# Seven plain pairs ahead of the block products, and modulation work spread anew, in a two-layer HGRN2 and gated-MLP backbone

## The chip, the cores and the metric

The kernel runs on one core of one Trainium2 chip. The metric is the device time of one execution in microseconds. TensorE (PE) multiplies matrices into eight PSUM banks, VectorE (DVE) and ScalarE (ACT) work elementwise, GpSimd (POOL) does a few small steps, and SyncE (SP) issues every DMA from one queue, in order. Each engine takes its instructions in the order in which they were laid down when the kernel was built; a semaphore makes an instruction wait for another engine or a DMA, and what stands behind it on its engine waits too.

## The reference, cut to what matters

Two layers work on 512 latent tokens of width 1024 and, in the first layer, on 256 context tokens as well. Each layer is a SwiGLU feed-forward, a token mixer (a bidirectional gated recurrence in the first, a chunked spatial MLP in the second), and another feed-forward. Every one of these has a modulated input and a modulated residual:

```
m = silu(cond) @ w_mod + b_mod                  # nine rows of 1024 for each layer and condition
h = x * (1 + m[3k+1]) + m[3k]                   # input of sub-layer k
g, u = split(h @ w_in);  y = (silu(g) * u) @ w_out
x = layer_norm(alpha * x + m[3k+2] * 0.5 * y)   # no 0.5 for the mixer
```

The context has a condition of its own (c_ctx), so a row of m that both streams use is computed for both conditions, "x" and "c". The feed-forward has 2816 hidden features, 22 blocks of 128. All products are in fp32, each made of three matmuls of rounded parts: high by high, high by low, low by high (L152, L153, L154).

## The kernel before

**Operands.** A weight tile is loaded to `raw` (3 buffers, 512 KB each) and split by ScalarE (L139, high part) and VectorE (L140, low part) into `w` (6 buffers). Token operands are split in the same way; `xa` holds the high and low part of all 768 tokens in one tile.

**Start.** Each of the eight 128-row slices k of the tokens needs two modulation dots (L171, one VectorE instruction of 1024 columns that multiplies a weight tile with the condition row and sums). As the slices come in, the three first feed-forward pairs (f = 0, 1, 2; a pair is the gate block and the up block of 128 hidden features) are summed in six PSUM banks (`products`, L1168). Behind them come the context's condition row, its tokens (1 MB) and its 16 dots, which use the same weight tiles (L1225 to L1231). Then the first three pairs are evacuated (`evac`, L1036: ScalarE silu, VectorE product to `h`, store to `hd` in DRAM), three more "plain" pairs are computed on the 512 latent tokens, and `context_operand` (L1234) scales and splits the context's tokens.

**Block products.** The other 16 pairs go over all 768 tokens in a form with seven instead of eight products (`by_sums`, L1053; `seven`, L669): gate and up, halves of the features and halves of the tokens are added and subtracted beforehand, the sums of the tokens are f4 to f7 (`sum_steps`, L1007), and every product is four slices of three matmuls with 384 columns. For the six plain pairs the 256 context tokens follow at the end.

**Output product.** `BothOut` (L1073) multiplies the stored pairs with the second weight. For each half of the 1024 output columns it goes over 11 units; a unit is one weight tile and two stored pairs (`hl`, 384 KB each), 36 matmuls of 512 columns. The tokens x come in at its start (six tiles, L1113). At the end it normalises, builds the operand of the recurrence, starts its values (psv) and stores x (L341, L342).

**Modulation.** The other rows of m are made on the side. `mod_task` (L173 on) is a generator: each step loads one 512 KB tile into `mraw` (2 buffers) and takes one dot for each condition; after eight steps it adds the bias, and a gate row (rows 2, 5, 8) is also transposed by TensorE (L187, pg) and stored. `mod_step(n)` adds n to a credit and runs as many steps as it holds; `made(key)` runs what is missing at once. Before, the queue holds rows (layer, row) (0, 2), (0, 4), (0, 3) for both conditions and (0, 5), (0, 7), (0, 6), (0, 8), (1, 2) for x: 64 steps. A block pair and a context pair give one step each, a unit of the output product two (its last units of either half give none), and L1280 makes the rest.

**Second layer's modulation.** The second feed-forward's output product makes rows (1, 1) and (1, 0) at one step a unit; the third's makes (1, 4), (1, 3), (1, 5) at 1.5.

**Pools.** SBUF is a stack of pools; a tile may take the place of an earlier pool's tile and then waits for that tile's last reader. `first` (the start's tiles) is closed before `hp` (silu, h) is opened in its place. In the second feed-forward `sp2` (rawu, e, sc of the block form) lies where `blocks` was, the tiles of token blocks from which f4 to f7 are summed.

The order on each engine comes from a scheduler when the kernel is built, by the program's order and its own estimate of times.

Of the kernel before, what the change touches and what calls it, by code (L numbers as in the profile page):

```python
# [11 lines left out]
F32 = mybir.dt.float32  # L12
# [30 lines left out]
NPLAIN = 6  # L43
# [31 lines left out]
def backbone_kernel(  # L75
# [905 lines left out]

    def new_xa():

        xa = xap.tile([P, 2, KD, TA], F32R, tag="xa", name="xa")
        return xa, xa[:, :, :, :T], xa[:, :, :, T:]
# [12 lines left out]
    class FeedBoth(Forms, FeedIn):  # L998
# [37 lines left out]
        def evac(self, hp, f, psg, psu, c0, c1):  # L1036
            c = slice(c0, c1)
            s = hp.tile([P, TA], F32, tag="silu", name="silu", bufs=1)
            nc.scalar.activation(s[:, c], psg[:, : c1 - c0], AF.Silu)
            h = hp.tile([P, TA], F32, tag="h", name="h", bufs=3)  # L1040
            nc.vector.tensor_tensor(h[:, c], psu[:, : c1 - c0], s[:, c], ALU.mult)
            nc.sync.dma_start(hd[f][:, c], h[:, c])
# [10 lines left out]
        def by_sums(self, hp, sp, f, early=None):  # L1053
            sc = sp.tile([P, 4, TS], F32, tag="sc", name="sc", bufs=1)
            s = hp.tile([P, TA], F32, tag="silu", name="silu", bufs=1)
            h = hp.tile([P, TA], F32, tag="h", name="h", bufs=3)
            pa, pe, pc, pb = self.seven(
                self.xa, sp, self.src(2 * f), self.src(2 * f + 1), [sc[:, i, :] for i in range(4)], early
            )
            if pb is not None:  # L1060
                nc.vector.tensor_tensor(s[:, TS:], sc[:, 3, :], pb, ALU.subtract)
            nc.vector.tensor_tensor(s[:, :TS], pa, sc[:, 0, :], ALU.add)
            nc.scalar.activation(s[:, :TS], s[:, :TS], AF.Silu)
            nc.vector.tensor_tensor(h[:, TS:], sc[:, 3, :], sc[:, 1, :], ALU.subtract)
            nc.vector.tensor_tensor(h[:, :TS], pe, sc[:, 2, :], ALU.add)
            if pb is not None:
                nc.scalar.activation(s[:, TS:], s[:, TS:], AF.Silu)
            else:
                nc.scalar.activation(s[:, TS:], pc, AF.Silu, scale=-1.0)
            nc.vector.tensor_tensor(h, h, s, ALU.mult)  # L1070
            nc.sync.dma_start(hd[f], h)
# [82 lines left out]
    with ExitStack() as e_sc:  # L1154
# [3 lines left out]
        f0.blk = early.enter_context(swap("blk")).tile([P, KD, TA], F32, name="blk")  # L1158
        with sbuf(name="first", bufs=1) as fp:
# [4 lines left out]
            xf = fp.tile([P, T], F32, name="xf")  # L1164
# [33 lines left out]
            for k in range(KD):  # L1198
# [20 lines left out]
                if k == 0:  # L1219
                    for _ in first:  # L1220
                        pass
                elif k < 4:
                    f0.load((2, 2, 1)[k - 1])
            products(KD - 1, staged)
            srow["c"] = silu_row(fp, "c")  # L1225
            nc.sync.dma_start(f0.blk[:, :, T:], ctxT.rearrange("k p t -> p k t"))
            for k in [*range(KD // 2, KD), *range(KD // 2)]:
                for ch in (1, 0):
                    mod_dot(fp, acc_c[:, k, ch : ch + 1], row(k, ch), srow["c"])
            ccols = const.tile([P, KD, 2], F32, name="ccols")  # L1230
# [3 lines left out]
        def context_operand():  # L1234
            for k in range(KD):
                ct = f0.blk[:, k, T:]
                nc.vector.tensor_scalar(ct, ct, ccols[:, k, 1:2], ccols[:, k, 0:1], ALU.mult, ALU.add)
                if k % 2:
                    ks = slice(k - 1, k + 1)
                    split(xmc[:, 0, ks, :], xmc[:, 1, ks, :], f0.blk[:, ks, T:])  # L1240
                    yield

        with sbuf(name="hp", bufs=1) as hp, sbuf(name="ru", bufs=1) as ru, sbuf(name="f47", bufs=1) as f47:
            for f in range(3):
                f0.evac(hp, f, f0.pss[2 * f], f0.pss[2 * f + 1], 0, T)
            ctx_steps = context_operand()
            for f in range(3, NPLAIN):
                f0.plain(hp, f, xm, 0, T)
                if f > 3:
                    for _ in range(2):  # L1250
                        next(ctx_steps, None)
            for _ in ctx_steps:
                pass
# [8 lines left out]
            for f in range(NPLAIN, NF):  # L1262
                f0.by_sums(hp, sp, f, steps if f == NPLAIN else None)
                if f == NPLAIN:
# [5 lines left out]
                    for l, ch in ((0, 5), (0, 7), (0, 6), (0, 8), (1, 2)):  # L1270
                        queue_mod(modq, srow, l, ch, ["x"])
                mod_step(1)
            for f in range(NPLAIN):
                f0.plain(hp, f, xmc, T, TA)
                mod_step(1)
        with bpools() as bp, sbuf(name="hl", bufs=1) as hl:
# [3 lines left out]
            for l, ch in ((0, 5), (0, 7), (0, 6), (0, 8), (1, 2)):  # L1280
                made((l, ch, "x"))


    with sbuf(name="hgo", bufs=1) as hgo, ExitStack() as late:
# [302 lines left out]
        with bpools() as bp:  # L1587
            xm = new_xm(xmp, "xm", T)
            n = KD * T
            flat = xap.tile([P, 2 * KD * TA], F32, tag="xa", name="blocks")[:, 2 * KD * TA - n :]  # L1590
# [7 lines left out]
    with sbuf(name="sp2", bufs=1) as sp, bpools() as bp, sbuf(name="hp2", bufs=1) as hp:  # L1598
# [11 lines left out]
        scraps(sp, 1, (1, 0))  # L1610
        op.run(bp, None, 1)
# [235 lines left out]
```

## Time and profile before

| What | Value |
|---|---|
| Time before, median of 3 runs (lowest to highest) | 2454.4 us (2454.2 to 2454.79) |
| The profiled execution's own time | 2452.35 us |
| Its span, first to last instruction | 2450.2 us |
| Granted TensorE clock, mean of the span | 0.993 |
| Share of the span busy: PE, DVE, ACT | 97%, 81%, 48% |
| Mean DMA rate over the span | 145 GB/s |

The page and the views group instructions by line, engine and tile names, "out<-in". In the list of waits a row has the waiting engine and tile, what released it, and the sum, the count and the longest of the waits. A timeline row has the start from the span's beginning, the duration, the engine, the line, the instruction and its tiles, and in brackets the idle time before it and its releaser. A row of windows has the stretch, its length, the busy time of PE, weight load, DVE, ACT and POOL (with counts), the granted clock, the busy share of the DMA engines and GB/s. Matmuls overlap, so the pace is read from start to start, not from a duration. Waits of engines other than TensorE cost nothing while TensorE is fed.

### The profile page before, as it was taken

Reading aid. Unit: us, or ns where it says so; the run is one execution under the profiler, and the core shown is the slowest. Engines: PE = TensorE matmul, PEld = TensorE weight load, DVE = VectorE, ACT = ScalarE, POOL = GpSimd, SP = SyncE. Lnnn points to the kernel's source line nnn. Section 1 sums busy time; section 2 is a strip of 40 time slices with the busy share of each in tenths; the row PEclk is TensorE's granted clock in tenths of the full one; section 3 lists DMA queues with packets and bytes.
Section 4 is the critical chain, followed back from the end, with each engine's and each line's share of the span. In section 5 each row is a group of like instructions: output and inputs, shape, how many; then the busy total and the mean of one; then the engine's idle time right before and its main releaser. Section 6 shows DMA issues by size and latency. Waiting matters only on the chain.

```text
span 2450.2 us, 37518 instructions
## 1 busy us (share of the span) xinstructions
PE 2383.5 (97%) x14787; PEld 2188.1 (89%) x14787; DVE 1985.2 (81%) x3173; ACT 1180.3 (48%) x1835; POOL 37.5 (2%) x57
## 2 busy tenths in 40 slices
PE   7899999996999999999999999999999999999998
PEld 5799998885889888899988999988999988999987
DVE  7987886866488886888796988898889877988785
ACT  4444442333354452555643655534566634555641
POOL 0000000000000000000000000000000000000000
PEclk9999999998999999999999999999999999999999
DMA  8444378953211113433474333474322365333452
GB/s 308 153 144 143 129 249 312 311 208 123 84 52 61 61 52 103 151 121 104 139 236 147 113 107 104 150 258 141 129 85 89 127 214 174 131 118 104 139 163 77
DMA packets 107889, 356.27 MB, mean 145 GB/s; under 512 B 12424, under 2 KB 14528, under 8 KB 107712
## 3 DMA queue, kind: packets, MB, share of 16 engines
q1 hardware_dynamic: 107712, 353.88, 42.8%
q8 instruction: 115, 1.88, 0.3%
q14 instruction: 62, 0.51, 0.1%
HBM read 332.57 MB, written 21.26 MB: 144 GB/s over the span
## 4 chain that ended last, share of the span: by engine, by line
PE 54%; DVE 3%; DMA 1%; ACT 0%; issue 0%; POOL 0%; SPq 0%; DVEq 0%; POOLq 0%
PE y L154 6%; PE y L153 6%; PE y L152 6%; PE psc L152 5%; PE psc L154 5%; PE psc L153 5%; PE pse L154 3%; PE pse L152 3%; PE pse L153 3%; PE psa L154 1%; PE psa L153 1%; PE psa L152 1%; PE pscs L1710 1%; PE pvc L154 1%; PE pvc L152 1%; PE pvc L153 1%
## 5 line engine op out<-in xcount | busy, mean ns | idle before, releaser
L139 ACT ACTIVATE w<-raw 128x1024 fp32r<-128x1024 f32 (+3 forms) x393 | 371.7, 949 | 359.3 <-DMA raw<-in_ffn_w_out 102.8
L140 DVE TENSOR_TENSOR w<-raw,w 128x1024 fp32r<-128x1024 f32 (+3 forms) x393 | 425.9, 1088 | 138.5 <-ACT w L139 137.7
L152 PE MATMUL y<-w,hs 128*128 128x512 f32 x984 | 383.4, 390 | 1.1 <-ACT hs L139 1.1
L154 PE MATMUL y<-w,hs 128*128 128x512 f32 x984 | 382.5, 389 | 1.6 <-DVE hs L140 1.6
L153 PE MATMUL y<-w,hs 128*128 128x512 f32 x984 | 382.7, 389 | 0.7 <-DVE w L140 0.7
L154 PEld LDWEIGHTS y<-w,hs 128*128 128x128 f32 x984 | 184.7, 188 | 40.8 <-DVE hs L140 2.0
L152 PEld LDWEIGHTS y<-w,hs 128*128 128x128 f32 x984 | 184.7, 188 | 39.5 <-ACT hs L139 1.5
L153 PEld LDWEIGHTS y<-w,hs 128*128 128x128 f32 x984 | 184.7, 188 | 39.0 <-DVE w L140 1.1
L152 PE MATMUL pse<-f,w 128*128 128x256 f32 (+1 forms) x688 | 202.0, 294 | 5.6 <-ACT sc L732 3.3
L152 PE MATMUL psc<-f,w 128*128 128x256 f32 (+1 forms) x688 | 201.8, 293 | 1.7 <-ACT sc L732 1.7
L154 PE MATMUL pse<-f,w 128*128 128x256 f32 (+1 forms) x688 | 202.3, 294 | 0.2 <-DVE w L140 0.2
L153 PE MATMUL pse<-f,w 128*128 128x256 f32 (+1 forms) x688 | 201.6, 293 | 0.0
L153 PE MATMUL psc<-f,w 128*128 128x256 f32 (+1 forms) x688 | 201.3, 293 | 0.0
L154 PE MATMUL psc<-f,w 128*128 128x256 f32 (+1 forms) x688 | 201.2, 292 | 0.0
L732 ACT ACTIVATE sc<-psc 128x256 f32<-128x256 f32 (+1 forms) x238 | 96.3, 404 | 150.8 <-PE psc L154 137.0
L152 PE MATMUL psc<-xm,w 128*128 128x256 f32 x548 | 156.1, 285 | 0.0
L154 PE MATMUL psc<-xm,w 128*128 128x256 f32 x548 | 155.1, 283 | 0.0
L153 PE MATMUL psc<-xm,w 128*128 128x256 f32 x548 | 155.0, 283 | 0.0
L140 DVE TENSOR_TENSOR w<-rawu,w 128x1024 fp32r<-128x1024 f32 x86 | 105.2, 1223 | 54.2 <-ACT w L139 53.6
L152 PEld LDWEIGHTS pse<-f,w 128*128 128x128 f32 x688 | 132.0, 192 | 6.4 <-ACT sc L732 4.0
L139 ACT ACTIVATE hs<-h 128x512 fp32r<-128x512 f32 x132 | 80.3, 628 | 113.9 <-PE y L154 98.7
L152 PEld LDWEIGHTS psc<-f,w 128*128 128x128 f32 x688 | 131.6, 191 | 2.5 <-ACT sc L732 2.5
(381 smaller groups left out, 6107.4 us busy)
## 6 DMA issues: line engine op xcount, KB each, us to landing
raw<-in_ffn_w_in SPq DMA_DIRECT2D x111, 512.0 KB, 4.4
raw<-in_ffn_w_out SPq DMA_DIRECT2D x88, 512.0 KB, 4.6
rawu<-in_ffn_w_in SPq DMA_DIRECT2D x76, 512.0 KB, 3.6
mraw<-in_mod_w SPq DMA_DIRECT2D x64, 512.0 KB, 4.3
rawu<-in_mod_w SPq DMA_DIRECT2D x64, 512.0 KB, 4.1
x<-x SPq DMA_DIRECT2D x36, 512.0 KB, 4.6
hl<-hd SPq DMA_DIRECT2D x44, 384.0 KB, 6.2
raw<-in_hg_wf SPq DMA_DIRECT2D x32, 512.0 KB, 3.6
```

Of the source, the lines that this page charges most:

```text
L139: latest_hi[0] = nc.scalar.activation(dst_hi, src, AF.Copy)
L140: latest[0] = nc.vector.tensor_tensor(dst_lo, src, dst_hi.bitcast(F32), ALU.subtract)
L152: nc.tensor.matmul(ps, ah, bh, start=start, stop=False, **kw)
L153: nc.tensor.matmul(ps, ah, bl, start=False, stop=False, **kw)
L154: return nc.tensor.matmul(ps, al, bh, start=False, stop=stop, **kw)
L732: self.copies.append(nc.scalar.activation(sc[i], ps[:, :N2], AF.Copy, scale=scale))
L1710: nc.tensor.matmul(pss[:, t * P : (t + 1) * P], vs[gi][:, t, ci * P : (ci + 1) * P], wsT[:, gi, :], start=True, stop=True,)
```

## The change

- Seven plain pairs instead of six (`NPLAIN`), so 15 block pairs and seven context pairs.
- The first three pairs are evacuated right behind `products`; the pool `hp` lies beside `first` for this, with two h buffers instead of three, and an unused tile goes. The context's 16 dots come behind the fourth and the fifth plain pair, eight each; its condition row and tokens are loaded ahead of the last slice. The context's scaling goes from VectorE to ScalarE, half behind the sixth and half behind the seventh plain pair.
- Modulation: block pairs give 1.25 steps each, from the second on; context pairs two. Row (1, 2) leaves this queue (56 steps stay) and is made in the second feed-forward, whose rate goes from 1 to 1.5.
- `xa` becomes two tiles of 24 KB, high and low (`Halves` makes them look like one); `blocks` takes the place of the first alone, at its start.
- In the second feed-forward the pool `bp` is opened ahead of `sp2`, so they change places in the stack.

```
-NPLAIN = 6
+NPLAIN = 7
...
-        xa = xap.tile([P, 2, KD, TA], F32R, tag="xa", name="xa")
+        xa = Halves(*(xap.tile([P, KD, TA], F32R, tag=f"xa{i}", name=f"xa{i}") for i in range(2)))
...
-            h = hp.tile([P, TA], F32, tag="h", name="h", bufs=3)
+            h = hp.tile([P, TA], F32, tag="h", name="h", bufs=2)
...
+        hp = e_hp.enter_context(sbuf(name="hp", bufs=1))
         with sbuf(name="first", bufs=1) as fp:
...
                 elif k < 4:
                     f0.load((2, 2, 1)[k - 1])
+                elif k == 6:
+                    srow["c"] = silu_row(fp, "c")
+                    nc.sync.dma_start(f0.blk[:, :, T:], ctxT.rearrange("k p t -> p k t"))
             products(KD - 1, staged)
-            srow["c"] = silu_row(fp, "c")
-            nc.sync.dma_start(f0.blk[:, :, T:], ctxT.rearrange("k p t -> p k t"))
-            for k in [*range(KD // 2, KD), *range(KD // 2)]:
-                for ch in (1, 0):
+            for f in range(3):
+                f0.evac(hp, f, f0.pss[2 * f], f0.pss[2 * f + 1], 0, T)
+            dots = [(k, ch) for k in [*range(KD // 2, KD), *range(KD // 2)] for ch in (1, 0)]
+            for f in range(3, NPLAIN - 2):
+                f0.plain(hp, f, xm, 0, T)
+                for k, ch in dots[:8]:
                     mod_dot(fp, acc_c[:, k, ch : ch + 1], row(k, ch), srow["c"])
+                dots = dots[8:]
...
-        def context_operand():
-            for k in range(KD):
+        def context_operand(k0):
+            for k in range(k0, k0 + KD // 2):
                 ct = f0.blk[:, k, T:]
-                nc.vector.tensor_scalar(ct, ct, ccols[:, k, 1:2], ccols[:, k, 0:1], ALU.mult, ALU.add)
+                nc.scalar.activation(ct, ct, AF.Identity, scale=ccols[:, k, 1:2], bias=ccols[:, k, 0:1])
...
-            for f in range(3, NPLAIN):
+            for f in (NPLAIN - 2, NPLAIN - 1):
                 f0.plain(hp, f, xm, 0, T)
-                if f > 3:
-                    for _ in range(2):
-                        next(ctx_steps, None)
-            for _ in ctx_steps:
-                pass
+                context_operand((f == NPLAIN - 1) * (KD // 2))
...
-                    for l, ch in ((0, 5), (0, 7), (0, 6), (0, 8), (1, 2)):
+                    for l, ch in ((0, 5), (0, 7), (0, 6), (0, 8)):
                         queue_mod(modq, srow, l, ch, ["x"])
-                mod_step(1)
+                if f > NPLAIN:
+                    mod_step(1.25)
             for f in range(NPLAIN):
                 f0.plain(hp, f, xmc, T, TA)
-                mod_step(1)
+                mod_step(2)
...
-            flat = xap.tile([P, 2 * KD * TA], F32, tag="xa", name="blocks")[:, 2 * KD * TA - n :]
+            flat = xap.tile([P, KD * TA], F32, tag="xa0", name="blocks")[:, : KD * T]
...
-    with sbuf(name="sp2", bufs=1) as sp, bpools() as bp, sbuf(name="hp2", bufs=1) as hp:
+    with bpools() as bp, sbuf(name="sp2", bufs=1) as sp, sbuf(name="hp2", bufs=1) as hp:
...
-        scraps(sp, 1, (1, 0))
-        op.run(bp, None, 1)
+        scraps(sp, 1, (1, 0, 2))
+        op.run(bp, None, 1.5)
```

More of the change, by code (lines that the diff above doesn't have):

```diff
@@ L980, in backbone_kernel, with __init__, __getitem__ @@
     xap = L0.enter_context(sbuf(name="xap", bufs=1))
+    class Halves:
+        def __init__(self, hi, lo):
+            self.parts = hi, lo
+        def __getitem__(self, at):
+            p, i, *rest = at
+            if isinstance(i, int):
+                return self.parts[i][(p, *rest)]
+            return Halves(*(t[(p, *rest)] for t in self.parts))
     def new_xa():
-        xa = xap.tile([P, 2, KD, TA], F32R, tag="xa", name="xa")
+        xa = Halves(*(xap.tile([P, KD, TA], F32R, tag=f"xa{i}", name=f"xa{i}") for i in range(2)))
         return xa, xa[:, :, :, :T], xa[:, :, :, T:]
@@ L1055, in by_sums @@
             s = hp.tile([P, TA], F32, tag="silu", name="silu", bufs=1)
-            h = hp.tile([P, TA], F32, tag="h", name="h", bufs=3)
+            h = hp.tile([P, TA], F32, tag="h", name="h", bufs=2)
             pa, pe, pc, pb = self.seven(
@@ L1152, in backbone_kernel @@
     xa, xm, xmc = new_xa()
-    with ExitStack() as e_sc:
+    with ExitStack() as e_sc, ExitStack() as e_hp:
         nc.scalar.preload_act_table(AF.Silu)
@@ L1163, in backbone_kernel @@
             bias = fp.tile([P, KD, 2], F32, name="bias")
-            xf = fp.tile([P, T], F32, name="xf")
             rows = xmp.tile([P, KD, D], F32, tag="xm", name="mrows")
@@ L1240, in context_operand @@
                     split(xmc[:, 0, ks, :], xmc[:, 1, ks, :], f0.blk[:, ks, T:])
[L1241 to L1246, printed above, removed]
-            for f in range(3, NPLAIN):
-                f0.plain(hp, f, xm, 0, T)
-                if f > 3:
-                    for _ in range(2):
-                        next(ctx_steps, None)
-            for _ in ctx_steps:
-                pass
+        with sbuf(name="ru", bufs=1) as ru, sbuf(name="f47", bufs=1) as f47:
+            for f in (NPLAIN - 2, NPLAIN - 1):
+                f0.plain(hp, f, xm, 0, T)
+                context_operand((f == NPLAIN - 1) * (KD // 2))
             flat = xmp.tile([P, 2, KD, T], F32R, tag="xm", name="f56").rearrange("p i k t -> p (i k t)")
@@ L1269, in backbone_kernel @@
                         queue_mod(modq, srow, 0, ch, ["x", "c"])
-                    for l, ch in ((0, 5), (0, 7), (0, 6), (0, 8), (1, 2)):
+                    for l, ch in ((0, 5), (0, 7), (0, 6), (0, 8)):
                         queue_mod(modq, srow, l, ch, ["x"])
-                mod_step(1)
+                if f > NPLAIN:
+                    mod_step(1.25)
             for f in range(NPLAIN):
                 f0.plain(hp, f, xmc, T, TA)
-                mod_step(1)
+                mod_step(2)
+        e_hp.close()
         with bpools() as bp, sbuf(name="hl", bufs=1) as hl:
@@ L1279, in backbone_kernel @@
             BothOut(ffn_units(0, 0), xa, hv).run(bp, hl, 2)
-            for l, ch in ((0, 5), (0, 7), (0, 6), (0, 8), (1, 2)):
+            for l, ch in ((0, 5), (0, 7), (0, 6), (0, 8)):
                 made((l, ch, "x"))
@@ L1588, in backbone_kernel @@
             xm = new_xm(xmp, "xm", T)
-            n = KD * T
-            flat = xap.tile([P, 2 * KD * TA], F32, tag="xa", name="blocks")[:, 2 * KD * TA - n :]
+            flat = xap.tile([P, KD * TA], F32, tag="xa0", name="blocks")[:, : KD * T]
             blocks.extend(flat.rearrange("p (i k t) -> p i k t", k=2, t=2 * P)[:, i] for i in range(KD))
```

## The prediction

> **What bounds the kernel now.** I read the page first: its shares, then who waited for whom on the matmul engine, longest first.
>
> ```profile
> span 2450.2 us, 37518 instructions
> PE 2383.5 (97%) x14787; PEld 2188.1 (89%) x14787; DVE 1985.2 (81%) x3173; ACT 1180.3 (48%) x1835; POOL 37.5 (2%) x57
> ```
>
> TensorE is busy for 97% of the span, so only its 66.7 us of idle time, its slow matmuls and the number of its columns can move the end. Its waits:
>
> ```profile
> PE pg L187 <- DVE acc_x L185: 19.8, 1, 19.8
> PE pse L152 <- ACT sc L732: 3.3, 1, 3.3
> PE psf L152 <- DVE h L1041: 3.1, 1, 3.1
> PE pse L152 <- ACT w L139: 2.3, 1, 2.3
> PE psf L152 <- ACT silu L1039: 1.9, 1, 1.9
> PE psc L152 <- ACT sc L732: 1.7, 1, 1.7
> PE y L152 <- ACT hs L139: 1.1, 1, 1.1
> PE y L153 <- DVE w L140: 0.7, 1, 0.7
> ```
>
> One wait holds 30% of all idle time. The timeline of TensorE at its place:
>
> ```profile
> 569.63 0.39 PE L152 MATMUL psv<-w,xa 128*128 128x512 f32 x1
> 576.88 0.39 PE L154 MATMUL psv<-w,xa 128*128 128x512 f32 x1
> 597.20 0.37 PE L187 MATMUL pg<-ident,acc_x 128*8 128x128 f32 x1 [19.82 <-DVE acc_x L185]
> 597.36 0.77 PE L152 MATMUL psv<-w,xa 128*128 128x512 f32 x1
> 602.43 0.39 PE L152 MATMUL psv<-w,xa 128*128 128x512 f32 x1
> ```
>
> From 569.63 to 576.88 there are 32 steps, so a 512-column matmul takes 0.2266 us. After the wait the 12 steps from 597.36 to 602.43 take 5.07 us instead of 2.72: slow matmuls that cost 2.35 more. What it waited for, on VectorE:
>
> ```profile
> 574.24 2.50 DVE L341 SCALAR_TENSOR_TENSOR x<-rb,x 128x512 f32<-128x512 f32 x4 [0.65 <-DMA rb<-in_ln_b]
> 576.65 1.22 DVE L171 SCALAR_TENSOR_TENSOR junk<-mraw,srow_x 128x1024 bf16<-128x1024 f32 x1
> 595.62 1.23 DVE L171 SCALAR_TENSOR_TENSOR junk<-mraw,srow_x 128x1024 bf16<-128x1024 f32 x1 [1.15 <-DMA mraw<-in_mod_w]
> 596.89 0.17 DVE L185 TENSOR_TENSOR acc_x<-acc_x,mbT 128x8 f32<-128x8 f32 x1
> ```
>
> These are eight modulation dots, left over when the first feed-forward ends. The budget says why: before, 16 block pairs and 6 context pairs give 22 steps, 17 units of the output product give 34: 56 steps for 64 tiles.
>
> **(a) The left-over dots: -22.1.** After: 14 x 1.25 + 7 x 2 = 31.5 steps, and 34 more, 65.5 for 56 tiles, since (1, 2) moves to the second feed-forward. TensorE's order before, with the value products (psv) around the transposes (pg):
>
> ```order
> L154 MATMUL psv_4813<-w_4677,xa_3232 128x512
> L187 MATMUL pg_4872<-ident_74,acc_x_4209 8x128
> L187 MATMUL pg_4912<-ident_74,acc_x_4878 8x128
> L152 MATMUL psv_4974<-w_4438,xa_3232 128x512
> L153 MATMUL psv_4974<-w_4438,xa_3232 128x512
> ```
>
> And after, at the same two value tiles:
>
> ```order
> L153 MATMUL psv_4829<-w_4693,xa0_3285 128x512
> L154 MATMUL psv_4829<-w_4693,xa1_3286 128x512
> L152 MATMUL psv_4943<-w_4454,xa0_3285 128x512
> L153 MATMUL psv_4943<-w_4454,xa0_3285 128x512
> L154 MATMUL psv_4943<-w_4454,xa1_3286 128x512
> ```
>
> No transpose stands between them: the wait has nothing left to wait for. 19.8 + 2.3 = 22.1. What is late next: the weights of the second half of the values. VectorE ends the store at 576.74 and needs two splits, done by 580; TensorE first has two tokens of 24 x 0.2266 = 5.4 us each. Nothing is late by this; I allow 0 to 3.
>
> **(b) The start: -10.0.** TensorE's waits and slow matmuls there:
>
> ```profile
> 66.96 0.50 PE L152 MATMUL psf<-xa,w 128*128 128x512 f32 x1 [1.90 <-ACT silu L1039]
> 75.78 0.50 PE L152 MATMUL psf<-xa,w 128*128 128x512 f32 x1 [3.08 <-DVE h L1041]
> 76.60 0.63 PE L152 MATMUL psf<-xa,w 128*128 128x512 f32 x1
> 79.99 0.39 PE L154 MATMUL psf<-xa,w 128*128 128x512 f32 x1
> 105.67 0.44 PE L152 MATMUL pse<-f,w 128*128 128x384 f32 x1 [3.29 <-ACT sc L732]
> 109.77 0.45 PE L152 MATMUL psc<-f,w 128*128 128x384 f32 x1 [1.75 <-ACT sc L732]
> ```
>
> Eight steps from 76.60 take 3.39 us instead of 1.81, so the part loses 1.9 + 3.1 + 1.6 + 3.3 + 1.7 = 11.6. VectorE before: the gated products h come behind all context dots (junk).
>
> ```order
> L171 SCALAR_TENSOR_TENSOR junk,acc_c<-mrows,srow_c 128x1024 x7
> L1231 TENSOR_TENSOR ccols<-acc_c,bias 128x16
> L1237 TENSOR_SCALAR blk<-blk,ccols 128x256 x2
> L1041 TENSOR_TENSOR h<-psf,silu 128x512
> L1237 TENSOR_SCALAR blk<-blk,ccols 128x256
> ```
>
> After:
>
> ```order
> L140 TENSOR_TENSOR xa_93<-blk,xa_92 128x512
> L171 SCALAR_TENSOR_TENSOR junk,acc_c<-mw,srow_c 128x1024 x2
> L1053 TENSOR_TENSOR h<-psf,silu 128x512
> L140 TENSOR_TENSOR w<-raw,w 128x1024 x2
> L1053 TENSOR_TENSOR h<-psf,silu 128x512
> ```
>
> The h that frees a PSUM bank now has two dots ahead of it since the operand, not sixteen: the first two waits go. For the last two, the seventh plain pair gives VectorE 48 x 0.2266 = 10.9 us more before the block products. I walked its new queue, with 1.22 for a dot or a weight split (1024 columns) and other widths in proportion: from the last operand split to the first block sum stand 14 dots, 9 weight splits, 6 h, 4 context splits and 4 sums, some 38 us and a wait for the sixth h, while TensorE has four plain pairs, 43.5, to do. So f5 is ready some 7 us ahead of its product; f7 and f4 come within a few tenths of theirs, since VectorE must still wait for the seventh pair's h in the middle of the sums. On ScalarE the copy of pse no longer stands behind the split of the fourth weight, which was what the wait of 3.3 came from. New is the second block pair: its split of e queues behind a subtraction that waits for psb, the first block pair's last product, so it comes about 1.3 late. And the 1.5 MB of context loads, issued ahead of the last operand rows now, add about 0.3. So 11.6 - 1.6 = 10.0; bounds 6 (three late operands of a microsecond or so more) and 11.6. The eight context scalings move to ScalarE, 48% busy over the span: hidden, and if not, they delay only the sums, by 8 x 0.4.
>
> **(c) The seventh plain pair: +2.1.** Pitches of 384 and 256 columns:
>
> ```profile
> 95.97 0.33 PE L152 MATMUL psa<-xa,w 128*128 128x384 f32 x1
> 97.88 0.33 PE L154 MATMUL psa<-xa,w 128*128 128x384 f32 x1
> 334.79 0.28 PE L153 MATMUL psf<-xa,w 128*128 128x256 f32 x1
> 335.99 0.28 PE L154 MATMUL psf<-xa,w 128*128 128x256 f32 x1
> ```
>
> 11 steps in 1.91 are 0.1736; 10 in 1.20 are 0.12. A block pair is 7 x 12 = 84 matmuls of 384: 14.58. A plain pair is 48 x 0.2266 + 48 x 0.12 = 16.64. The difference is certain, as TensorE is the bound.
>
> **(d) The output product's third unit: +6.0.** Two mod steps a context pair (1 before) put weight tiles on the DMA queue where the output product's loads went ahead before. SP before, from the last context pair:
>
> ```order
> L1042 DMA hd<-h 128x256
> L145 DMA raw<-in_ffn_w_out 128x1024
> L177 DMA mraw<-in_mod_w 128x1024
> L1113 DMA x<-in_x 128x1024 x4
> L1113 DMA x<-in_ctx_tok 128x1024 x2
> L1085 DMA hl<-hd 128x768 x3
> ```
>
> After:
>
> ```order
> L1054 DMA hd<-h 128x256
> L177 DMA mraw<-in_mod_w 128x1024 x2
> L1125 DMA x<-in_x 128x1024 x4
> L1125 DMA x<-in_ctx_tok 128x1024 x2
> L191 DMA gr_5_x<-mrow 8x128
> L145 DMA raw<-in_ffn_w_out 128x1024
> L1097 DMA hl<-hd 128x768 x2
> ```
>
> Before, weights for six units and half of the third unit's activations stood ahead of the 3.1 MB of x; now two units do, and the third unit comes behind x and behind a store that waits for a transpose.
>
> ```profile
> L154 PE MATMUL psf<-xa,w x192: 280/335/628, 12.8 to 367.3; 128*128 128x512 f32 x96, 128*128 128x256 f32 x96
> 374.20 1.96 SPq L1113 DMA_DIRECT2D x<-in_x  x4
> 387.79 2.77 ACT L139 ACTIVATE hs<-hl 128x768 fp32r<-128x768 f32 x3 [11.02 <-DMA hl<-hd]
> 375.00:381.00 6.00, 6.00 (x28) 4.99 (x27) 1.23 (x1) 1.06 (x1) 0.00 (x0) 1.00 0.96 358
> 381.00:387.00 6.00, 6.00 (x28) 4.95 (x28) 0.00 (x0) 0.00 (x0) 0.00 (x0) 1.00 1.03 418
> ```
>
> A weight tile and a modulation tile are 512 KB, an activation pair two of 384:
>
> ```profile
> mraw<-in_mod_w SPq DMA_DIRECT2D x64, 512.0 KB, 4.3
> hl<-hd SPq DMA_DIRECT2D x44, 384.0 KB, 6.2
> ```
>
> A unit is 36 x 0.2266 = 8.16 us, so the third starts 16.3 after the last context matmul (367.3). x was issued 6.9 after it, its successor landed at 20.5. After, two modulation tiles, six x, a weight and two activations must pass: 1.05 + 3.15 + 0.52 + 0.79 = 5.5 MB, at the 388 GB/s of the last two rows 14.2 us. Counted from the same 6.9 that is 21, and with a split 22; the other way, the old landing of 20.5 plus 0.92 MB more is 22.6. The third unit wants them at 16.3. So the wait is 4.7 to 6.3; I take 5.5, plus 1.6 of slow matmuls (as at 76.60), less the 1.1 that goes: +6.0. Bounds -1 and +12.
>
> Such slowness is a clock that needs activity: the Trainium skill (TensorE: Matmul & The Clock Gate, What's actually happening) has it halve after an idle window of about 3.4 us. The trace disagrees in part, since 3.08 sufficed; by the page the 1.6 in (b) would not be there to win, while a wait of 5.5 would be charged up to 1.7.
>
> **(e) Pools swapped: -0.4.** The rawu load no longer waits for the blocks.
>
> ```profile
> 1015.93 0.42 DVE L778 TENSOR_TENSOR silu<-psa,sc 128x256 f32<-128x256 f32 x1 [0.78 <-PE psa L154]
> 1016.72 0.69 DVE L713 TENSOR_TENSOR e<-raw,rawu 128x512 f32<-128x512 f32 x1 [0.36 <-DMA rawu<-in_ffn_w_in]
> ```
>
> But e stands behind L778, which waits for psa. Of the 2.3 only 0.36 goes; bounds 0 and 2.3.
>
> **(f) Modulation in the second feed-forward at 1.5: +0.7.** The third runs so already and waits 0.7 (the last wait listed); bounds 0 and 2.
>
> Two tiles for the operand, and two h buffers instead of three (pairs 14.6 us apart, their store a few): 0 to 1, taken 0.
>
> Sum: -22.1 - 10.0 + 2.1 + 6.0 - 0.4 + 0.7 = -23.7. The profiled execution took 2452.35, 2.0 under the median 2454.4; the change goes onto the median: **2430.7**.
>
> **Rivals.** *DMA sets the pace (0.18).* A context pair now asks for 4 x 0.52 + 0.13 = 2.23 MB in 5.76 us, 387 GB/s.
>
> ```profile
> 346.00:388.00 42.00, 41.56 (x268) 37.76 (x267) 27.98 (x42) 13.79 (x18) 0.00 (x0) 1.00 0.95 342
> ```
>
> At 342 with the queues 95% busy it takes 6.52: 7 x 0.76 = 5.3, and the third unit some 3.5 later: 2439.5. Against it: weights are split two pairs ahead. The Trainium skill (DMA: Bandwidth & Descriptors, Where 436 GB/s comes from) puts the limit for loads from HBM at about 358 GB/s; the row of 418 disagrees. By 358 the pairs would lose 3.3.
>
> *No new wait in (d) (0.15).* x lands sooner or the queue is empty by then: 2430.7 - 7.1 = 2423.6.
>
> *Slower: loads and dots in series (0.03).* Each output unit's loads stand behind two mod tiles in two buffers; if they start only when the dots are done, a unit takes the time of its 2.36 MB and then that of its splits and dots.
>
> ```profile
> 388.00:430.00 42.00, 41.32 (x182) 34.09 (x183) 31.37 (x44) 13.96 (x16) 0.00 (x0) 1.00 0.85 282
> ```
>
> At 282 GB/s that is 8.4, and with 3 x 1.22 and two splits of 768 columns (0.92 each) 5.5 more: 13.9 for 8.16. The 13 units with modulation lose 75, less the wait of (d): about 2500. It decides from 10.2 a unit, where 13 x 2 eat the 23.7 won and more. Against it: in this very row two steps a unit ran with TensorE busy for 41.3 of 42 us.
>
> *The change doesn't do it (0.01).* Steps still left over: 2452. The order above speaks against it.
>
> **Numbers.** Forecast 0.63: the costs' bounds give 2425 to 2437. 2421 to 2440 takes in the second rival and most of the first. About 0.2%, 4.9 us, is what a measurement tells: faster 0.96, same 0.01, slower 0.03.
>
> **What would show it.** Right: no wait over 1 us at pg; the waits on silu and h gone before the block products; a wait of 4 to 7 at the third output unit, on hs or w; 96 more 256- and 512-column matmuls. Wrong: a wait among the value products, several waits in the output product, or (d) without one.

## The result, and the profile after

The changed kernel takes 2429.33 us (median of four executions, 2427.94 to 2429.66) beside 2454.6 before: a ratio of 0.9892, 95% interval 0.9875 to 0.9909. Forecast were 2430.7. The profiled execution took 2427.94, 24.4 less than the profiled one before; its span is 2426.2, 24.0 less.

The page of the changed kernel, its first lines:

```profile
span 2426.2 us, 37551 instructions
PE 2383.7 (98%) x14799; PEld 2185.7 (90%) x14799; DVE 1976.5 (81%) x3159; ACT 1180.7 (49%) x1839; POOL 35.1 (1%) x57
```

TensorE is as long busy as before (2383.5) and idle for 42.5 us instead of 66.7. Its longest waits:

```profile
PE psf L152 <- ACT xa L1223: 10.9, 1, 10.9
PE y L152 <- ACT hs L139: 6.2, 2, 5.9
PE psf L152 <- ACT w L139: 6.0, 3, 4.2
PE pse L152 <- ACT w L139: 3.3, 2, 1.8
PE psv L152 <- DVE xa L140: 1.8, 1, 1.8
```

The wait of 19.8 at pg has gone, those on silu, h and sc too; the longest one that remains beside the first loads is new, at the output product. Within 548 to 622 us, where the values are made, the list of waits now has a single line, the last of these five.

Where the time went is read from the timeline of TensorE: the start of the first matmul of each stage in both kernels, and the stage's length.

| Stage begins with | start before | start after | its length: before, after | difference | forecast |
|---|---|---|---|---|---|
| start, plain pairs | 0 | 0 | 93.86, 98.26 | +4.40 | (b) and (c) |
| block products | 93.86 | 98.26 | 239.02, 220.45 | -18.57 | (b) and (c) |
| context pairs | 332.88 | 318.71 | 34.55, 40.69 | +6.14 | (b) and (c) |
| output product | 367.43 | 359.40 | 181.12, 189.27 | +8.15 | (d) +6.0 |
| normalising, values | 548.55 | 548.67 | 94.68, 72.54 | -22.14 | (a) -22.1 |
| recurrence | 643.23 | 621.21 | 342.95, 342.11 | -0.84 | none |
| second feed-forward's start | 986.18 | 963.32 | 26.62, 26.62 | 0 | none |
| its block products | 1012.80 | 989.94 | 206.49, 205.34 | -1.15 | (e) -0.4 |
| its output product | 1219.29 | 1195.28 | 121.43, 122.48 | +1.05 | (f) +0.7 |
| all behind, to the last matmul | 1340.72 | 1317.76 | 1100.72, 1099.91 | -0.81 | none |

The sum is -23.77; forecast was -23.7. The first three rows together are -8.03, and (b) and (c) were -10.0 + 2.1 = -7.9. Among them, the plain part grew by 4.40 for a pair of 48 x 0.2266 = 10.88, so it lost 6.5 less; a block pair less is -14.58, so the block products lost 4.0 less. The context pairs grew by 48 x 0.12 = 5.76 for one pair more and by 0.39 ahead of the output product's first matmul. What is left in the block products is one wait, at the second block pair:

```profile
116.55 0.44 PE L152 MATMUL pse<-f,w 128*128 128x384 f32 x1 [1.46 <-ACT w L139]
116.83 0.33 PE L153 MATMUL pse<-f,w 128*128 128x384 f32 x1
```

It is the one that was forecast at 1.3. ScalarE's timeline ahead of it:

```profile
112.86 1.06 ACT L165 ACTIVATE srow_x<-srow_x 128x1024 f32<-128x1024 f32 x1 [1.40 <-DMA srow_x<-in_cond]
114.08 1.06 ACT L165 ACTIVATE srow_c<-srow_c 128x1024 f32<-128x1024 f32 x1 [0.15 <-DMA srow_c<-in_cond]
115.46 1.04 ACT L139 ACTIVATE w<-e 128x1024 fp32r<-128x1024 f32 x1
```

The number of matmuls follows as well: each line of psf<-xa has 224 instead of 192, so 96 more.

```profile
L152 PE MATMUL psf<-xa,w 128*128 128x512 f32 (+1 forms) x224 | 75.1, 345 | 17.0 <-ACT xa L1223 10.9 <-ACT w L139 6.0
```

The new wait of (d): the third unit on TensorE, and the eight steps behind it.

```profile
382.91 0.80 PE L152 MATMUL y<-w,hs 128*128 128x512 f32 x1 [5.93 <-ACT hs L139]
383.51 0.73 PE L153 MATMUL y<-w,hs 128*128 128x512 f32 x1
...
386.61 0.63 PE L153 MATMUL y<-w,hs 128*128 128x512 f32 x1
387.04 0.44 PE L154 MATMUL y<-w,hs 128*128 128x512 f32 x1
```

Eight steps take 4.13 us instead of 1.81. The first three take 2.0 of it, since the operands' low parts are only being made, as VectorE's timeline shows; the five behind them go at 0.427, half speed.

```profile
382.16 1.23 DVE L140 TENSOR_TENSOR w<-raw,w 128x1024 fp32r<-128x1024 f32 x1 [8.31 <-ACT w L139]
383.31 1.82 DVE L140 TENSOR_TENSOR hs<-hl,hs 128x768 fp32r<-128x768 f32 x2
```

The DMA queue ahead of it (start, duration of the issue, line, tile):

```profile
360.55 0.90 SPq L1097 DMA_DIRECT2D hl<-hd  x2
365.28 0.32 SPq L1054 DMA_DIRECT2D hd<-h  x1
365.70 0.88 SPq L177 DMA_DIRECT2D mraw<-in_mod_w  x2
367.18 2.36 SPq L1125 DMA_DIRECT2D x<-in_x  x4
369.59 1.04 SPq L1125 DMA_DIRECT2D x<-in_ctx_tok  x2
373.87 0.30 SPq L191 DMA_DIRECT2D gr_x<-mrow  x1
374.21 0.33 SPq L145 DMA_DIRECT2D raw<-in_ffn_w_out  x1
374.59 0.90 SPq L1097 DMA_DIRECT2D hl<-hd  x2
```

The third unit's weight and activations (the last two rows) stand behind x and behind the gate row's store, which holds the queue from 370.63 to 373.87. They are issued 15 us after the first matmul of the output product (359.40); the third unit wants them at 16.3.

### The profile page after: what moved, and what is told of

The parts are those of the page before. It is cut to its first block, busy times and chain, and to the rows that moved or that the text cites. A ratio compares the mean times of both kernels' runs of the same rounds, so it can differ in the third digit from the quotient of the medians.

```text
span 2426.2 us, 37551 instructions
## 1 busy us (share of the span) xinstructions
PE 2383.7 (98%) x14799; PEld 2185.7 (90%) x14799; DVE 1976.5 (81%) x3159; ACT 1180.7 (49%) x1839; POOL 35.1 (1%) x57
## 4 chain that ended last, share of the span: by engine, by line
PE 88%; DVE 6%; DMA 3%; issue 1%; ACT 1%; POOL 0%; SPq 0%; DVEq 0%; POOLq 0%; ACTq 0%
PE y L154 8%; PE y L153 8%; PE y L152 8%; PE psc L152 7%; PE psc L154 7%; PE psc L153 7%; PE pse L154 4%; PE pse L152 4%; PE pse L153 3%; PE psf L152 2%; PE psf L154 2%; PE psf L153 2%; PE psa L153 2%; PE psa L152 2%; PE psa L154 2%; PE psq L154 1%
## 5 line engine op out<-in xcount | busy, mean ns | idle before, releaser
L152 PE MATMUL pse<-f,w 128*128 128x256 f32 (+1 forms) x680 | 198.9, 292 | 3.5 <-ACT w L139 3.3
L154 PE MATMUL pse<-f,w 128*128 128x256 f32 (+1 forms) x680 | 199.0, 293 | 0.3 <-DVE w L140 0.2
L152 PE MATMUL psc<-f,w 128*128 128x256 f32 (+1 forms) x680 | 198.9, 293 | 0.0
L154 PE MATMUL psc<-f,w 128*128 128x256 f32 (+1 forms) x680 | 198.6, 292 | 0.0
L153 PE MATMUL psc<-f,w 128*128 128x256 f32 (+1 forms) x680 | 198.5, 292 | 0.0
L153 PE MATMUL pse<-f,w 128*128 128x256 f32 (+1 forms) x680 | 198.5, 292 | 0.0
L152 PEld LDWEIGHTS pse<-f,w 128*128 128x128 f32 x680 | 130.0, 191 | 4.2 <-ACT w L139 3.8
L154 PEld LDWEIGHTS pse<-f,w 128*128 128x128 f32 x680 | 130.0, 191 | 0.9 <-DVE w L140 0.7
```

The lines of the kernel that those rows point to most:

```text
L152: nc.tensor.matmul(ps, ah, bh, start=start, stop=False, **kw)
L153: nc.tensor.matmul(ps, ah, bl, start=False, stop=False, **kw)
L154: return nc.tensor.matmul(ps, al, bh, start=False, stop=stop, **kw)
```

## The experiments

Times are medians; each session also ran the kernel before: 2455.87 in the first, 2454.77 in the second, 2454.02 in the third.

**Context pairs at one step.**

```
-                mod_step(2)
+                mod_step(1)
```

> The changed kernel with one modulation step for each context pair instead of two. The steps still suffice: 14 x 1.25 + 7 + 34 = 58.5 for 56 tiles. Theory (the new wait in the output product comes from the order of the DMA queue: two modulation tiles a context pair push the third unit's weight behind the 3.1 MB of x and behind the gate row's store): the 5.9 us wait at the third unit falls to 0 to 1.5, its 3.4 us of slow matmuls go too, and no wait returns at the end of the first feed-forward. 2429.3 - 7 = 2422.3, range 2420.5 to 2424.5. Rival (the 3.1 MB of x alone stop the third unit, with or without the modulation tiles): the wait stays at 4 to 6, 2427 to 2430. Second rival (the steps are now too few late in the output product): a wait of some us before the values' second half, 2426 or more.

Measured: 2419.63, ratio 0.9861 (0.9845 to 0.9877); 9.7 us under the changed kernel and a little below the theory's range. The output product takes 179.85, 9.4 less, and the list of waits has no line for it. Both rivals fall: x alone does not stop the third unit, and 58.5 steps are enough. The queue shows what differs. Six hl pass ahead of x here, four in the changed kernel (the last two of them at 360.55 above); the fifth and the sixth are these:

```profile
358.31 0.38 SPq L1097 DMA_DIRECT2D hl<-hd  x1
359.03 0.33 SPq L177 DMA_DIRECT2D mraw<-in_mod_w  x1
360.08 0.32 SPq L1097 DMA_DIRECT2D hl<-hd  x1
...
366.62 1.75 SPq L1125 DMA_DIRECT2D x<-in_x  x4
```

**x behind the first four units.** In `BothOut.run`, ahead of the loop that loads x:

```
+            self.lead(0, 4, nmod)
             for t in range(nt):
                 xt = bp.tile([P, D], F32, tag="x", name="x", bufs=nt)
```

> The changed kernel with the loads of x issued behind the loads of the output product's first four units instead of ahead of them; two steps a context pair stay, so the bytes are the same and only the order of the queue is another. Theory (order of the queue): the third unit does not wait; at most 0 to 2 us at the fifth, whose loads now stand behind x. 2420.5 to 2424.5, middle 2422.5. Rival (bytes: the DMA engines cannot move this part's bytes in its time, whatever the order): a wait of 4 to 6 moves to the fifth unit, 2427 to 2430.

Measured: 2427.62 (2423.68 to 2430.16). The theory's time is missed, the rival's is met: the output product takes 187.64. The third unit does not wait; the fifth does, the first one whose loads stand behind x:

```profile
397.18 0.80 PE L152 MATMUL y<-w,hs 128*128 128x512 f32 x1 [3.68 <-ACT hs L139]
```

The order decides which unit waits. The wait itself lies between the theory's 0 to 2 and the rival's 4 to 6, so the run doesn't say how much of it is bytes. The profiled execution was the slowest of the four, and the second feed-forward's output product took 125.66 in it, 3.2 more than in the changed kernel.

**The old modulation in the changed kernel.**

```
-                    for l, ch in ((0, 5), (0, 7), (0, 6), (0, 8)):
+                    for l, ch in ((0, 5), (0, 7), (0, 6), (0, 8), (1, 2)):
...
-                if f > NPLAIN:
-                    mod_step(1.25)
+                mod_step(1)
...
-                mod_step(2)
+                mod_step(1)
...
-        scraps(sp, 1, (1, 0, 2))
-        op.run(bp, None, 1.5)
+        scraps(sp, 1, (1, 0))
+        op.run(bp, None, 1)
```

> The changed kernel with the modulation as before: row (1, 2) back in the first queue, one step for each of the 22 pairs, rate 1 in the second feed-forward. All else of the change stays (seventh pair, context dots, pools, two operand tiles). Theory (terms add up: the left-over dots cost 22.1, and the new wait at the third unit, measured 8.2, belongs to the modulation's spread, the 0.7 to 1 of the second feed-forward as well): a wait of 18 to 21 at pg, about 1 at the third unit, none before the block products but 1.5 in the second block pair. 2429.3 + 22.1 - 8.2 - 1 = 2442.2, range 2440 to 2445. Rival (the start's gain needs the first block pair's freedom from modulation): 2 to 5 more, 2445 to 2448. Second rival (the third unit's wait is due to the seventh context pair): the wait stays, 2449 to 2452.

Measured: 2441.64, inside the theory's range. The wait at pg is back (20.4), the output product takes 179.71 without a wait, the start loses as little as in the changed kernel.

```profile
PE pg L187 <- DVE acc_x L185: 20.4, 1, 20.4
```

**The new modulation alone.** In the kernel before, row (1, 2) leaves the first queue and the second feed-forward gets rate 1.5; nothing else.

```
-                    for l, ch in ((0, 5), (0, 7), (0, 6), (0, 8), (1, 2)):
+                    for l, ch in ((0, 5), (0, 7), (0, 6), (0, 8)):
...
-        scraps(sp, 1, (1, 0))
-        op.run(bp, None, 1)
+        scraps(sp, 1, (1, 0, 2))
+        op.run(bp, None, 1.5)
```

> The kernel before with one edit: row (1, 2) leaves the first queue and is made in the second feed-forward at rate 1.5. 16 + 6 + 34 = 56 steps for 56 tiles, one a pair as before. Theory: -22.1 for the left-over dots, +0.7 to +1 for the rate; the start's waits on silu, h and sc stay, and the third unit's stays near 1. 2454.5 - 21.3 = 2433.2, range 2431 to 2436. Rival (with no credit to spare the last row ends in the value products, whose transpose then waits): a wait of 2 to 8 there, 2435 to 2441.

Measured: 2432.07 (2430.53 to 2434.81), a time within the theory's range; no wait among the value products but the old one of 1.3. The third unit's wait was expected to stay near 1; it is 4.3, the first of these lines:

```profile
PE y L152 <- ACT hs L139: 4.3, 1, 4.3
PE pse L152 <- ACT sc L732: 4.2, 1, 4.2
PE psf L152 <- ACT silu L1039: 1.8, 1, 1.8
PE psf L152 <- DVE h L1041: 1.6, 1, 1.6
```

**The kernel before, once more.** No edit.

> The kernel before once more, for its profile alone. In the kernel with the new modulation alone the third unit of the output product waited 4.35 us, though its DMA queue and all engines have the same order up to there as before. Theory (that wait depends on how fast the DMA engines happen to run in a profiled execution): it is somewhere from 0 to 5 here, the start's waits stay within 1 us of 1.9, 3.1, 3.3 and 1.7, the left-over dots at 19 to 21. Time 2452 to 2457. Rival (1.1 is the value of this order, and 4.35 came from something else in that kernel): 0.9 to 1.4.

Measured: 2453.74; the profiled execution 2457.91. On the third unit the theory holds: the same order gave 1.1 in the profile that the prediction read, and here 3.8. Of the start's waits the one of 1.7 is missing here; the other three are within 0.1.

```profile
PE pg L187 <- DVE acc_x L185: 20.2, 1, 20.2
PE y L152 <- ACT hs L139: 3.8, 1, 3.8
PE pse L152 <- ACT sc L732: 3.3, 1, 3.3
PE psf L152 <- DVE h L1041: 3.2, 1, 3.2
PE psf L152 <- ACT silu L1039: 1.8, 1, 1.8
```

The windows of 340 to 388 us show a difference, first of the earlier profile:

```profile
340.00:388.00 48.00, 47.56 (x318) 43.76 (x317) 33.24 (x49) 16.36 (x22) 0.00 (x0) 1.00 0.94 340
```

And of this one:

```profile
340.00:388.00 48.00, 48.00 (x325) 44.57 (x323) 33.74 (x51) 16.54 (x21) 0.00 (x0) 1.00 0.92 315
```

The DMA engines moved 315 instead of 340 GB/s, and x was issued at 377.39 instead of 374.20. Why they moved less is not shown. The output product takes 186.57 here, 185.86 in the kernel with the new modulation alone, 181.12 in the profile of the prediction.

**Six plain pairs.**

```
-NPLAIN = 7
+NPLAIN = 6
...
-            for f in range(3, NPLAIN - 2):
+            for f in range(3, 5):
...
-            for f in (NPLAIN - 2, NPLAIN - 1):
-                f0.plain(hp, f, xm, 0, T)
-                context_operand((f == NPLAIN - 1) * (KD // 2))
+            f0.plain(hp, NPLAIN - 1, xm, 0, T)
+            for k0 in (0, KD // 2):
+                context_operand(k0)
```

> The changed kernel with six plain pairs again: the sixth pair is the last ahead of the block products, all eight context scalings and splits come behind it, eight context dots each behind the fourth and fifth pair as before this edit. Theory (the seventh pair costs 2.1 and is worth it, since VectorE needs its 10.9 us to finish the sums of the blocks): without it the sums come 5 to 9 us late, as waits on f or on ScalarE's splits at the first block pair. 2429.3 - 2.1 + 8 = 2435, range 2431 to 2440. Rival (the new place of the dots is all that helps; the seventh pair only costs): 2427, range 2425 to 2428.5.

Measured: 2435.02. The theory holds. Waits of 80 to 120 us:

```profile
PE pse L152 <- ACT w L139: 4.2, 2, 3.1
PE psc L152 <- ACT w L139: 3.3, 1, 3.3
PE pse L154 <- DVE w L140: 0.8, 1, 0.8
```

Counted as steps above the pitches of the prediction, from 50 to 130 us, this kernel loses 13.6, the kernel before 12.7 to 13.4 and the changed one 2.3. The new place of the dots wins nothing by itself; it moves the waits from silu and h to the first block pairs. VectorE works there without a pause from 85.20 to 110.0, and the split of e behind the wait of 3.3 starts on ScalarE right behind VectorE's subtraction (L718). The gain comes with the seventh pair's 10.9 us.

**The pools as before.**

```
-    with bpools() as bp, sbuf(name="sp2", bufs=1) as sp, sbuf(name="hp2", bufs=1) as hp:
+    with sbuf(name="sp2", bufs=1) as sp, bpools() as bp, sbuf(name="hp2", bufs=1) as hp:
```

> The changed kernel with the two pools of the second feed-forward in their old places; the order of the instructions is the same on every engine. Theory (the pools are worth nothing here, since the subtraction behind the load stands behind one that waits for psa; the 206.4 us of the kernel with the old modulation and the new pools and the 205.1 of the kernel with the new modulation alone and the old pools speak for it): 2429.3, within 1.5, the wait for the second pair's weight 1.8 to 2.3. Rival (the swap made the 1.1 us that the second feed-forward's block products are shorter by): 2430.5 to 2432.

Measured: 2431.71 (2429.61 to 2433.49), above the theory's range and within the rival's; its profiled execution took 2430.17. The stage speaks against the rival: 205.34 us for the second feed-forward's block products, as with the new pools. The wait at the second pair is 2.2 instead of 1.8. The time alone is inconclusive, since it overlaps that of the changed kernel run again (below); in the stage that they touch the pools are worth nothing that shows.

**Context pairs at 1.5 steps.**

```
-                mod_step(2)
+                mod_step(1.5)
```

> The changed kernel with 1.5 modulation steps for each context pair instead of 2: three or four tiles fewer ahead of the output product. With two steps the third unit lost 9.8 us, with one nothing. Theory (bytes: each tile of 512 KB is some 1.35 us of the queue at 388 GB/s, and the wait falls by as much): a wait of 0 to 2 at the third unit, 2421.5, range 2419.5 to 2424. Rival (two tiles in two buffers stall the queue in every context pair, and half a tile fewer makes no such stall better than by half): a wait of 2.5 to 5, 2424 to 2428.

Measured: 2421.97, as the theory of bytes has it; the output product takes 180.30, without a wait on hs. Fewer tiles also bring six activation loads ahead of x, so the run doesn't tell bytes from order; the run with two steps for the last three pairs (below) bears on which of the two counts.

**The changed kernel, once more.** No edit.

> The changed kernel once more, for its profile. Theory (with four of the activation loads ahead of x the third unit always stops): a wait of 5 to 7 at the third unit with 3 to 4 of slow matmuls behind it, the left-over dots' wait absent, the second block pair's wait 1.3 to 1.6. 2428 to 2431. Rival (5.9 was a chance of one profile, as 1.1 was for the kernel before): anything from 1 to 8.

Measured: 2430.86 (2429.31 to 2431.36). The third unit stops here as well, with 2.3 lost in slow steps behind it instead of the 3 to 4 expected; the time and the other waits are the theory's:

```profile
PE y L152 <- ACT hs L139: 5.6, 1, 5.6
PE psv L152 <- DVE xa L140: 1.8, 1, 1.8
PE pse L152 <- ACT w L139: 1.4, 1, 1.4
```

**One step for four context pairs, two for the last three.**

```
-                mod_step(2)
+                mod_step(1 + (f > 3))
```

> The changed kernel with one modulation step for the first four context pairs and two for the last three: 10 tiles, about as many as at 1.5 a pair (10 or 11), but crowded in front of the output product. When the kernel is built, six activation loads come ahead of x on the queue, as at rates 1 and 1.5; at rate 2 it is four, in the kernel before five. Theory (what counts is whether both activations of the third unit stand ahead of x): no wait over 1 there, as at 1.5: 2422, range 2419.5 to 2424. Rival (what counts is how many tiles pass in the last pairs): a wait of 3 to 6, 2424.5 to 2430.

Measured: 2423.96 (2421.72 to 2427.2), within the theory's range at its upper end. No unit waits over 0.4, so the rival falls. The output product still takes 181.72, 1.9 more than at one step a pair, in late steps of the fourth and fifth unit. Six activation loads stand ahead of x here, as at rates 1 and 1.5 and with the old modulation (no wait at the third unit); five in the kernel before and with the new modulation alone (1.1 to 4.3), four in the changed kernel, with the old pools and with six plain pairs (5.9 and 5.6, 5.4, 4.3). The third unit needs the fifth and the sixth.

**Eight plain pairs, at one step a context pair.**

```
-NPLAIN = 7
+NPLAIN = 8
...
-                mod_step(2)
+                mod_step(1)
```

> The changed kernel with eight plain pairs and one step a context pair. Theory (seven are enough for VectorE; an eighth costs 2.1 and can only take away the 1.3 to 1.6 us wait of the second block pair, which is not due to a lack of time for the sums but to one subtraction behind psb, so it stays): 2419.6 + 2.1 = 2421.7, range 2420.5 to 2424. Rival (the sums are still short of time with seven): the wait goes, 2419 to 2420.3.

Measured: 2422.17, 2.5 over the same kernel with seven. The time is the theory's; its reason is not, since the second block pair's wait did shrink, from 1.3 to 0.5: 0.8 won, 2.1 spent. That the medians differ by 2.5 and not by 1.3 lies within the spread of either (2421.41 to 2424.22 here).

**One step a context pair, and 1.42 in the second feed-forward.**

```
-                mod_step(2)
+                mod_step(1)
...
-        op.run(bp, None, 1.5)
+        op.run(bp, None, 1.42)
```

> The changed kernel with one step a context pair and 1.42 instead of 1.5 in the second feed-forward (17 x 1.42 = 24.1 for 24 tiles). Theory: the first edit makes 2419.6 as measured; the second spreads the same 24 tiles over the last two units too, and takes away at most the 1.1 to 1.4 us by which that output product is longer than at rate 1: 2418.2 to 2420. Rival (the extra time there comes with the eight tiles however they are spread): 2419.6, within 0.7.

Measured: 2418.69, ratio 0.9853 (0.9838 to 0.9868), the lowest of all. The second feed-forward's output product takes 122.37 instead of 122.81. That both rates together beat the first alone is not shown: 0.9 us lies within the spread of either (2418.02 to 2426.85 and 2418.31 to 2422.5).

## Why the prediction was right, point by point

The sum came out at -23.77 for -23.7, and that closeness is in part luck: (d) and (f) came out 2.5 higher than forecast, while (e), the recurrence and the part behind the second feed-forward came out 2.4 lower, the last two without a term and within what they vary between executions. Two slips stand in the prediction's working. In (d), 0.92 MB at 388 GB/s are 2.4 us, so the second way to the landing gives 22.9 and a wait of 6.6, not 22.6 and 6.3; the value taken, 5.5, stays between. And the bounds of its terms, added up, reach from about 2420 to 2446; 2425 to 2437 holds only if they don't all fall on one side.

**(a) The left-over dots, -22.1: right, and shown.** Measured -22.14. With the old modulation the wait comes back at 20.4; with the new modulation alone it goes, and nothing is late in its place.

**(b) and (c), the start and the seventh pair, -10.0 and +2.1: right in sum and in kind.** Measured -8.03 for -7.9. That VectorE needs the seventh pair's time was the reason given, and the run with six pairs shows it: without that pair, (b) is about nothing. The forecast 1.3 at the second block pair measured 1.46. Its cause is in part another than the prediction's. The subtraction behind psb (L1073) starts at 113.30 without any idle time of VectorE before it, and e is complete at 114.45; ScalarE splits it only from 115.46, since the two condition rows of the modulation, for whose loads it had waited 1.40 and 0.15, and a silu stand ahead of the split. An eighth pair took most of the wait away; no run moves the condition rows alone.

**(d) The third output unit, +6.0: place and cause right, size and base off.** Against the profile that the prediction read the price was 8.15. The parts, by steps: 5.93 for the wait (5.5 forecast) and 0.15 by which the modelled end of the matmul before it lies behind its pitch; 2.3 for eight slow steps (1.6 forecast); 1.4 at the first unit, whose operands are a little late too (none forecast); less 1.4 that the kernel before lost (1.1). That is 8.4 by steps and 8.15 by the stage; 0.39 of the first unit's loss lies ahead of its first matmul, in the row of the context pairs. Of the 2.3, eight steps at half speed are 1.6, as forecast; 0.7 are the low parts that VectorE makes late in the first three steps. What the sum left out is what else comes late with the loads: the low parts, and the first unit. The Trainium skill (TensorE: Matmul & The Clock Gate, What's actually happening) has a halved clock last until TensorE has been busy for a window of about 3.4 us; half of that, 1.7, is an estimate of its price from that figure. The steps at 0.427 agree with the halving. The other flaw is the base. The wait of 1.1 was one execution's; the same order gave 3.8 and 4.3 in two others, and against their output products of 186.57 and 185.86 the price of (d) is 2.7 to 3.4. The profile with 1.1 was 2.25 below the median of its kernel (2454.6) and the one with 3.8 was 4.2 above (2453.74), so the price against a usual execution lies between 2.7 and 8.15 and is not known better. That the medians differ by 25.3 and the profiled executions by 24.4 goes the same way.

Bytes and order were both part of the reason as the prediction put it. Order is shown: in the seven profiles with six or more activations ahead of x the third unit doesn't wait on them, in the seven with five or four it does. That bytes count as well is argued only: with x moved back the wait went on to the fifth unit, as both would have it. In the context pairs bytes were not what held the queue up. From 319 to 361 us the DMA engines of the changed kernel moved 286 GB/s, 302 at one step a pair, and up to 420 later (last section); the queue itself waited 28.6 us for VectorE there (12.5 for h, 7.8 for weight splits, 4.6 for modulation dots, 3.7 for other small steps) and 2.3 for a transfer. Behind x the engines were at 415 to 420 GB/s, so there the 3.1 MB did stand in the way. What the gate row's store, which holds the queue for 3.2, adds to the wait no run parts.

**(e) The pools, -0.4: right to expect next to nothing.** The stage got 1.15 shorter, but with the old pools as well (205.34 and 205.11), and not with the new pools and the old modulation (206.44). The order of the instructions in that stage is the same with either modulation. What differs is the clock behind one wait: it was halved there in the three profiles with the old modulation and in none of the eleven others (last section). Why the new modulation moves that wait to another place on the clock's grid stays open.

**(f) Rate 1.5, +0.7.** Measured +1.05 in the changed kernel. In its repeat and the variants with rate 1.5 it is 1.05 to 2.2, with 2.7 (six plain pairs) and 4.2 (x later) in two; the bound of 2 was too low.

**Unforeseen:** -0.84 in the recurrence and -0.81 behind the second feed-forward, where nothing was forecast. One wait of 1.6 on hs, in the output product that begins at 1959 us of the kernel before, is absent when that kernel is run again, and over all runs the recurrence takes between 341.8 and 342.95 and the part behind the second feed-forward between 1099.2 and 1101.9: a spread between executions.

**The rivals.** *DMA sets the pace* did not come: the context pairs took 40.69 / 7 = 5.81, not 6.52. *No new wait in (d)* did not come either, but a kernel without it exists, and is better than that rival's 2423.6. *Loads and dots in series* did not come for TensorE.

The largest thing that the prediction missed is none of its terms: the new wait buys nothing. At one step a context pair 14 x 1.25 + 7 + 34 = 58.5 steps still cover 56 tiles. With that rate, or with the old modulation, the changed kernel's output product takes 179.7 to 179.9: not only the new wait is absent, but also the one that the kernel before has (1.1 and 3.8 in its two profiles). The changed kernel without its modulation (2441.64) is 14.2 under the kernel before, the modulation alone (2432.07) 23.8, both by the first session's 2455.87; together 38.0. The whole change has 25.3, at one step a pair 36.2. Of the 12.7 between 38.0 and 25.3, 9.4 were lost in the output product (189.27 beside 179.85); the other 3.3 are not traced to a stage, and compare medians of different sessions.

## What to carry to other kernels

When two edits each remove waits, look for what they ask of the same queue: here steps raised from one to two in a stretch where DMA was busy for 85 to 95% cost 9.7 us and were not needed. Count the budget (steps given, steps needed) before a rate is raised, and look which unit's loads then stand behind a large transfer. Before a term is worked out as a difference from a wait of one profile, read that wait in a second execution, above all where the DMA engines are busy for over 90%.

## What the runs showed of the hardware

How long matmuls stay slow is not read from the wait ahead of them alone. In the second feed-forward the same instruction waits 1.83 us with the old and with the new modulation. In the changed kernel the matmuls of 256 columns behind it run at 0.12:

```profile
994.81 0.39 PE L152 MATMUL pse<-f,w 128*128 128x256 f32 x1 [1.83 <-ACT w L139]
...
998.05 0.28 PE L153 MATMUL pse<-f,w 128*128 128x256 f32 x1
998.17 0.28 PE L154 MATMUL pse<-f,w 128*128 128x256 f32 x1
```

In the changed kernel with the old modulation they fall to 0.21 two microseconds later:

```profile
1008.25 0.38 PE L152 MATMUL pse<-f,w 128*128 128x256 f32 x1 [1.83 <-ACT w L139]
...
1011.53 0.41 PE L154 MATMUL pse<-f,w 128*128 128x256 f32 x1
1011.75 0.41 PE L152 MATMUL pse<-f,w 128*128 128x256 f32 x1
```

The granted clock (the last but two of the numbers in a row of windows) shows when this happens. In each of the 14 profiles it changes only at points of a grid of 3.413 us, to within 5 ns; the grid lies elsewhere in each execution. In the changed kernel the changes are at 380.302, 387.129 and 2421.472, 2 and 596 times 3.4133 apart. Its windows on this grid at the third unit:

```profile
376.89:380.30 3.41, 0.09 (x1) 0.00 (x0) 0.00 (x0) 0.00 (x0) 0.00 (x0) 1.00 1.02 415
380.30:383.72 3.42, 0.81 (x2) 0.57 (x2) 1.56 (x2) 2.59 (x3) 0.00 (x0) 0.50 1.03 420
383.72:387.13 3.41, 3.34 (x8) 2.25 (x9) 3.38 (x5) 0.50 (x2) 0.00 (x0) 0.50 0.96 371
387.13:390.54 3.41, 3.41 (x17) 2.77 (x16) 3.18 (x5) 2.18 (x3) 0.00 (x0) 1.00 0.95 286
```

The clock was halved behind a window in which TensorE was nearly idle, and came back behind one in which it was busy. So 2.6 of the 6.83 us at half speed fell into the wait itself, and cost nothing. The waits of 1.83 to 2.3 at the instruction above, in all 14 profiles, follow the grid too: where the wait ended 1.42, 2.29 or 2.92 us behind a grid point (the three with the old modulation), the clock was halved at the next point; where it ended 0.11 to 1.28 behind one (the other eleven), it was not. How much of the wait lies in one window does not decide it alone: 1.72 us of the changed kernel's lie in one (991.29 to 994.70) that no halving followed, 1.42 of the other kernel's in one (1006.82 to 1010.24) that was followed by it, and twelve matmuls start in either. What tips it is not shown. So slow steps can follow 1.8 us of waiting, or not, and a sum can only give them a range. The Trainium skill (TensorE: Matmul & The Clock Gate, What's actually happening) has the activity counted in windows that run freely, whatever the program does; the grid agrees with it, and by it the same wait may fall into one window or across two.
